# Weight sums of a Strassen-type product: from GpSimd instructions to an adding transfer

## Chip, cores and metric

One NeuronCore of a Trainium2 chip runs the whole program. The metric is the device time of one execution in microseconds (us). All data are float32; the products are made of float32r parts.

## What is computed

A trunk of four residual layers on 512 tokens of 1024 features, each layer a mixer followed by a SwiGLU feed-forward network, and one RMS norm at the end:

```python
for i in range(DEPTH):                       # 4 layers
    h = rmsnorm(x, norm_mix_g[i])
    m = short_conv(h) | spatial_gating(h) | retention(h)   # kinds 0, 1, 2, then 0 again
    x = x + m
    h = rmsnorm(x, norm_ffn_g[i])
    x = x + (silu(h @ w_gate) * (h @ w_up)) @ w_down       # 1024 -> 2816 -> 1024
return rmsnorm(x, final_norm_g)
```

The short convolution's input weights are 1024 x 3072, the gate and up weights 1024 x 2816 each.

## The kernel before

Every operand of a product is split into two float32r parts, high and low, and a product is three matmuls: high times high, high times low, low times high. `split` (lines 155 to 158) makes the parts: ScalarE casts to the high part, VectorE subtracts it from the source.

**Seven products for eight.** The convolution's input products and the gate and up products of the feed-forward networks use Winograd's form of Strassen's scheme: the weight matrix and the activations are cut in quarters, and seven products of quarters, or of sums of quarters, stand for eight. `columns7` makes 256 output features (a "chunk") that way: 7 parts of 12 matmuls, 84 matmuls of 256 columns. There are 104 such chunks: 20 in the two convolutions and 84 in the four feed-forward networks. The first chunk of each stage is made plainly by `columns4`, without sums.

**Weights.** `prepare7` (lines 114 to 140) prepares a chunk in two halves. For a half, SyncE loads 512 KB into a `raw` buffer (line 121; 4 buffers). The quarters lie in the order a11, a12, a22, a21. GpSimd makes three sums (lines 131 to 133), s1 = a21 + a22, s2 = s1 - a11 and s4 = a12 - s2, and VectorE makes s3 = a11 - a21 (line 134), all in a `sums` buffer (2 buffers, so one chunk). Then the three plain quarters of `raw` and the four sums are split (lines 157 and 158) into buffers of the pools `w7` and `wp`, which have four buffers each for either part, two chunks' worth. So the cast of a half waits until TensorE is done with the chunk before last, and the next sums wait until VectorE's subtraction has freed the `sums` buffer.

**Activations.** `operand_sums` (lines 381 to 396) makes the sums of quarters t1 to t4 of the activations for two blocks of features, four times in each stage that needs them: t1 and t3 by VectorE, t2 and t4 by GpSimd. `operand` (lines 366 to 376) scales and splits a block of x right after `leave` has added to it (line 422).

**Outcome.** `columns7` gathers the seven parts in three PSUM banks; ScalarE copies intermediate ones out (lines 227 to 243) and VectorE adds them (line 224). GpSimd also adds up squares for the norms (lines 302 to 307).

**Order.** A framework's scheduler orders each engine's instructions at build time by its own timeline; every engine then runs its list in order, and a transfer on SyncE's or GpSimd's queue waits in order too. `weights` prepares up to four chunks ahead, but at most one of the seven-part kind. In a feed-forward network the hidden blocks are made in four groups, (0,2), (2,5), (5,8), (8,11), a gate and an up chunk for each block; the down projection of one group (`leave`, eight blocks of 512-column matmuls) runs after the first gate chunk of the next. So four to six seven-part chunks follow each other between two down projections. In a convolution there are nine or eleven, with one small `leave` in between.

Of the kernel before, what the change touches and what calls it, by code (L numbers as in the profile page):

```python
# [17 lines left out]
P = 128  # L18
# [3 lines left out]
NB = D // P            # feature blocks of the residual stream  # L22
NT = T // P            # token blocks
FF = 2816
NF = FF // P
H = T // 2             # tokens of half the sequence
FF_PARTS = ((0, 2), (2, 5), (5, 8), (8, 11))  # pairs of hidden blocks, by part of an FFN
# [8 lines left out]
LAG = 3                # blocks of u that are ahead of the mixing of v  # L36
SOON = 100             # instructions that urgent ones may pass in the scheduler's order
BEGUN = 4              # blocks whose products begin before the last of their operands are ready
AHEAD = 4              # weight chunks prepared ahead of their matmuls


class Kernel:
# [18 lines left out]
    @contextmanager  # L61
    def dense(self):
        """Memory of the layers whose products take seven parts."""
        with (
            self.tc.tile_pool(name="w7", bufs=4, reuse_waits="tile") as self.w7,
            self.tc.tile_pool(name="sums", bufs=2, reuse_waits="tile") as self.sums,
            self.tc.tile_pool(name="hid", bufs=6, reuse_waits="tile") as self.hid,
            self.tc.tile_pool(name="own", bufs=1, reuse_waits="tile") as self.own,
        ):
            self.eye = self.diagonal(self.own.tile([P, P], F32, name="eye"))  # L70
            yield
        self.w7 = None

    @contextmanager
    def mixed(self):
        """Memory of the other layers."""
        with self.tc.tile_pool(name="blk", bufs=29, reuse_waits="tile") as self.blk:
            yield

# [17 lines left out]
    def plan7(self, src, plain=False):  # L97
        """Two blocks of columns, for columns4 if plain, else for columns7."""
        self.chunks.append((src, 0, plain))
# [14 lines left out]
    def prepare7(self, i):  # L114
        """Two blocks of columns, as the seven left operands of Winograd's form of Strassen's product."""
        nc = self.nc
        src, _, plain = self.chunks[i]
        out = [[] for _ in range(8)]
        for half in range(2):
            raw = self.raw.tile([P, NB // 4, 4, P], F32, tag="raw", name=f"raw{i}{half}")  # L120
            nc.sync.dma_start(raw, src[half])
            if plain:
                h, l = (self.wp.tile([P, NB // 4, 4, P], F32R, tag=part, name=f"w{part}{i}{half}") for part in "hl")
                self.split(raw, h, l)
                for j in range(4):
                    out[j] += [(h[:, k, j], l[:, k, j]) for k in range(NB // 4)]
                continue
            sums = self.sums.tile([P, NB // 4, 4, P], F32, tag="sums", name=f"sums{i}{half}")
            a11, a12, a22, a21 = (raw[:, :, j] for j in range(4))
            s1, s2, s3, s4 = (sums[:, :, j] for j in range(4))  # L130
            nc.gpsimd.tensor_add(s1, a21, a22)  # L131
            nc.gpsimd.tensor_sub(s2, s1, a11)  # L132
            nc.gpsimd.tensor_sub(s4, a12, s2)  # L133
            nc.vector.tensor_sub(s3, a11, a21)  # L134
            for x, n, first, pool in ((raw, 3, 0, self.w7), (sums, 4, 3, self.wp)):
                h, l = (pool.tile([P, NB // 4, n, P], F32R, tag=part, name=f"w{part}{i}{half}{n}") for part in "hl")
                self.split(x[:, :, :n], h, l)
                for j in range(n):
                    out[first + j] += [(h[:, k, j], l[:, k, j]) for k in range(NB // 4)]
        return out  # L140
# [14 lines left out]
    def split(self, src, h, l):  # L155
        """A float32 tile as two float32r tiles whose sum it is."""
        self.nc.scalar.copy(h, src)  # L157
        self.nc.vector.tensor_sub(l, src, h.bitcast(F32))  # L158
# [7 lines left out]
    def product(self, ps, terms, first=True, last=True, more=False):  # L166
        """ps (+)= sum of lhsT.T @ rhs over (lhs_h, lhs_l, rhs_h, rhs_l), the last term's at the end;
        more: added to a finished sum."""
        nc = self.nc
        seq = []  # L170
        for lh, ll, rh, rl in terms[:-1]:
            seq += [(lh, rh), (lh, rl)]
        seq += [(ll, rh) for lh, ll, rh, rl in terms[:-1]]
        lh, ll, rh, rl = terms[-1]
        seq += [(lh, rh), (lh, rl), (ll, rh)]
        for i, (x, y) in enumerate(seq):
            nc.tensor.matmul(  # L177
                ps, x, y, start=first and i == 0, stop=last and i == len(seq) - 1, skip_group_check=more
            )

    def columns(self, name, acts):
        """One block of output features (on partitions), for all tokens."""
# [14 lines left out]
    def begin(self, name, acts):  # L197
        """The start of columns(), with the weights of the rest."""
# [5 lines left out]
    def columns7(self, name, then, hold=False):  # L204
        """Two blocks of output features of the residual stream. then() gets them as [P, 2 * T], when the
        next product is under way."""
# [21 lines left out]
        part(c5, 3, xt, 0, True)  # L228
# [3 lines left out]
        part(c1, 4, xt, 1, False)  # L232
# [5 lines left out]
        part(c1, 5, xt, 2, False)  # L238
        add(y[:, 2 * H : 3 * H], c1, m5)

        def end():
            part(c1, 2, xt, 3, False)
            nc.scalar.copy(y[:, 3 * H :], c1)
# [4 lines left out]
    def columns4(self, name, then, hold=False):  # L248
        """The same by four products of blocks, for which the sums of the operand needn't be ready."""
# [16 lines left out]
    def finish(self, hold=False):  # L266
        """The rest of the last columns7, and what is done with its outcome (and those before it) unless on hold."""
# [8 lines left out]
    def rows(self, name, acts):  # L276
        """512 output features for each block of tokens (on partitions)."""
# [17 lines left out]
    def squares(self, src, add=None):  # L295
        """Running sum, over feature blocks, of the squares."""
# [12 lines left out]
    def rsqrt(self, ps, out, t):  # L309
        """out = ps ** -0.5, with a Newton step."""  # L310
# [7 lines left out]
    def scale_of(self, mean, r, t, *sums):  # L318
        """Each token's 1 / rms, on all partitions."""
# [8 lines left out]
    def diagonal(self, eye):  # L328
        """The matrix that mean_d is the inverse of, on vectors: D on the diagonal."""
# [8 lines left out]
    def scale_of_tokens(self, total):  # L338
        """Each token's 1 / rms, with tokens on partitions: a column for 128 of them."""
# [12 lines left out]
    def spread(self, r, t):  # L352
        """The same on all partitions, in PSUM."""
# [7 lines left out]
    def scale_in_psum(self):  # L361
        """Each token's 1 / rms, on all partitions."""
        return self.spread(self.scale_of_tokens(self.sum), self.hid.tile([P, 2 * T], F32, tag="hid", name="rs")[:, :T])

# [1 line left out]
    def operand(self, m, g):  # L366
        """x's block m as a part of the next product's operand."""
# [13 lines left out]
    def operand_sums(self, k, g):  # L381
        """The sums of quarters among the seven right operands, of two blocks of features."""
# [8 lines left out]
        nc.vector.tensor_sub(t1, b12, b11)  # L391
        nc.gpsimd.tensor_sub(t2, b22, t1)
        nc.vector.tensor_sub(t3, b22, b12)
        nc.gpsimd.tensor_sub(t4, b21, t2)
# [3 lines left out]
    def blocks(self):  # L398
        """The operand by single blocks of features."""
        return [(h[:, s], l[:, s]) for h, l in self.xs for s in (slice(0, T), slice(T, 2 * T))]  # L400

    def leave(self, acts, g, seven=False, final=True, midway=None, before=[], begun=()):
        """x += acts @ w; the next norm's gain is g. before: acts that begun products have already."""
# [26 lines left out]
    def end(self, acts):  # L430
        """The last layer's acts @ w on top of x, and the last norm, by halves of the tokens."""
# [37 lines left out]
    def last_norm(self, t, m):  # L469
        """Two blocks of features of half the tokens."""  # L470
# [14 lines left out]
    def normed(self, y, r):  # L485
        """y / rms, for two blocks"""
# [94 lines left out]
    def sgu(self, j, g, seven):  # L581
# [3 lines left out]
        # v, tokens on partitions  # L585
# [37 lines left out]
        # the causal mixing matrices, transposed: [s, group, t]  # L623
# [12 lines left out]
        # u, features on partitions, gated with the mixed v  # L636
# [32 lines left out]
    def retention(self, j, g, seven):  # L669
# [12 lines left out]
        for hd in range(HEADS):  # L682
# [28 lines left out]
            # scores, keys on partitions; of the last keys only 128 queries are left  # L711
# [79 lines left out]
    def plan_out(self, w, lo, hi):  # L791
        """All blocks of columns, of the blocks lo to hi of rows."""
# [84 lines left out]
def columns_by_two(w):  # L877
    """[n, K, M] as [n, M / 256, 2, P, K / 4 * 2]: two blocks of columns, half the rows at a time,
    rows on partitions, by pairs of blocks of rows."""
    n, k, m = w.shape  # L880
    w = w.reshape(n, 2, k // (4 * P), 2, P, m // (2 * P), 2, P).transpose(0, 5, 1, 4, 2, 6, 3, 7)
    return np.ascontiguousarray(w.reshape(n, m // (2 * P), 2, P, k // (4 * P), 4, P)[..., [0, 1, 3, 2], :])


def columns_first(w, parts=1):
    """[n, K, M] as [n, M / P, (parts,) P, K / P / parts * P]: one block of columns, rows on partitions."""
# [6 lines left out]
def rows_first(w):  # L893
    """[n, K, M] as [n, M / T, K / 256, P, 2 * T]: two blocks of rows of 512 columns."""
# [5 lines left out]
def tables():  # L900
    """Rotary angles and decays, by position and head alone."""
# [10 lines left out]
def by_partition(v):  # L912
    """[..., D] as [P, ... * D / P]."""
# [46 lines left out]
```

## Time and profile before

| | |
|---|---|
| time, median of 3 runs | 2485.07 us (2484.79 to 2485.66) |
| span of the profiled execution, first to last instruction | 2484.2 us |
| around the span (median less span; the profiled execution has no other time of its own) | 0.9 us |
| TensorE busy | 2417.6 us, 97% |
| VectorE busy | 1836.7 us, 74% |
| ScalarE busy | 1132.3 us, 46% |
| GpSimd busy | 890.0 us, 36% |
| mean granted TensorE clock | 0.994 of 2.4 GHz |

In rows of the profile, PE is TensorE, PEld its weight loads, DVE VectorE, ACT ScalarE, POOL GpSimd, and SP SyncE, which issues the loads. L134 is line 134 of the kernel. A name such as `wl<-sums,wh` says which tile is written from which. Times of instructions are in nanoseconds where the row says mean ns, all others in microseconds.

### The profile page before, as it was taken

The numbers are of one execution on the slowest core, as the hardware profiler recorded it, in microseconds if no ns is written. First come the engines' busy times: TensorE is split into PE (matmuls) and PEld (weight loads), VectorE is DVE, ScalarE is ACT, GpSimd is POOL, SyncE is SP. The second block draws the span as 40 slices with busy tenths as digits, with TensorE's granted clock in tenths as the row PEclk, the third lists the DMA queues.
The fourth block names the chain that finished last, engine by engine and source line by source line (L and its number), as shares of the span: only waits on it lengthen the run. The fifth ranks groups of instructions, "written<-read, shape, count | busy, mean of one in ns | idle before, by whom it ended". The sixth has DMA issues, their size and how long they took to land.

```text
span 2484.2 us, 37622 instructions
## 1 busy us (share of the span) xinstructions
PE 2417.6 (97%) x14892; PEld 2179.7 (88%) x14892; DVE 1836.7 (74%) x2236; ACT 1132.3 (46%) x1638; POOL 890.0 (36%) x788
## 2 busy tenths in 40 slices
PE   7999999999999999999999999999999899999998
PEld 6988989988888899998888888799999788889988
DVE  7988878763757887767565465988767898978776
ACT  6455445443324544534333334545435545545443
POOL 5536533520101643442000000834433744733530
PEclk9999999999999999999999999999999999999999
DMA  4141333334332233233223131233234124133231
GB/s 154 62 145 53 116 111 95 97 115 119 94 103 92 68 111 122 88 97 122 95 72 94 60 123 58 91 107 115 85 98 132 52 69 153 52 119 103 85 112 59
DMA packets 78832, 242.09 MB, mean 97 GB/s; under 512 B 8768, under 2 KB 12864, under 8 KB 78656
## 3 DMA queue, kind: packets, MB, share of 16 engines
q1 hardware_dynamic: 77568, 238.65, 30.3%
q8 instruction: 116, 1.90, 0.3%
q10 hardware_dynamic: 1088, 1.05, 0.1%
q14 instruction: 60, 0.49, 0.1%
HBM read 237.56 MB, written 2.10 MB: 96 GB/s over the span
## 4 chain that ended last, share of the span: by engine, by line
PE 75%; DVE 16%; issue 5%; ACT 2%; POOL 1%; DMA 0%; SPq 0%; DVEq 0%; ACTq 0%; POOLq 0%
PE out L177 26%; PE pu L177 16%; PE pg L177 15%; PE pv L177 7%; DVE wl L158 6%; PE pc L177 2%; PE q L177 2%; PE k L177 2%; PE pb L177 2%; DVE sums L134 2%; DVE puy L512 1%; PE pz L177 1%; DVE xl L375 1%; PE po L177 1%; DVE pgy L488 1%
## 5 line engine op out<-in xcount | busy, mean ns | idle before, releaser
L157 ACT CAST wh<-raw 128x768 fp32r<-128x768 f32 (+3 forms) x500 | 425.1, 858 | 572.5 <-PE out L177 193.5
L158 DVE TENSOR_TENSOR wl<-raw,wh 128x768 fp32r<-128x768 f32 (+3 forms) x500 | 557.6, 1134 | 136.7 <-ACT wh L157 136.3
L131 POOL TENSOR_TENSOR sums<-raw 128x256 f32<-128x256 f32 x208 | 243.3, 1170 | 795.8 <-DMA raw<-in_ffn_w_up 360.7
L157 ACT CAST wh<-sums 128x1024 fp32r<-128x1024 f32 x208 | 212.2, 1046 | 182.6 <-POOL sums L133 78.0
L177 PE MATMUL out<-hidl,wh 128*128 128x512 f32 (+1 forms) x736 | 278.3, 380 | 0.0
L158 DVE TENSOR_TENSOR wl<-sums,wh 128x1024 fp32r<-128x1024 f32 x208 | 260.9, 1279 | 22.1 <-ACT wh L157 18.8
L177 PE MATMUL out<-hidh,wh 128*128 128x512 f32 (+1 forms) x736 | 274.6, 381 | 0.0
L133 POOL TENSOR_TENSOR sums<-raw,sums 128x256 f32<-128x256 f32 x208 | 230.1, 1107 | 10.4
L132 POOL TENSOR_TENSOR sums<-sums,raw 128x256 f32<-128x256 f32 x208 | 217.9, 1048 | 10.6
L177 PE MATMUL pg<-xl,wh 128*128 128x256 f32 (+1 forms) x672 | 201.9, 316 | 9.6 <-DVE xl L375 9.6
L422 DVE TENSOR_TENSOR x<-out,x 128x512 f32<-128x512 f32 x192 | 130.2, 683 | 107.0 <-PE out L177 105.9
L177 PE MATMUL out<-hidh,wl 128*128 128x512 f32 (+1 forms) x736 | 205.4, 380 | 0.0
L177 PE MATMUL pg<-xh,wh 128*128 128x256 f32 (+1 forms) x672 | 200.9, 315 | 0.0
L177 PE MATMUL pu<-tl,wh 128*128 128x256 f32 x704 | 185.4, 284 | 5.1 <-DVE tl L158 5.1
L177 PE MATMUL pu<-xl,wh 128*128 128x256 f32 (+1 forms) x656 | 190.0, 306 | 0.0
L177 PE MATMUL pu<-xh,wh 128*128 128x256 f32 (+1 forms) x656 | 189.7, 306 | 0.0
L134 DVE TENSOR_TENSOR sums<-raw 128x256 f32<-128x256 f32 x208 | 153.3, 752 | 44.1 <-DMA raw<-in_ffn_w_up 37.9
L177 PE MATMUL pu<-th,wh 128*128 128x256 f32 x704 | 185.5, 285 | 0.0
L177 PE MATMUL pg<-th,wh 128*128 128x256 f32 x640 | 168.3, 284 | 6.9 <-DVE pgy L224 6.9
L177 PE MATMUL pg<-tl,wh 128*128 128x256 f32 x640 | 167.3, 283 | 0.0
L177 PEld LDWEIGHTS out<-hidl,wh 128*128 128x128 f32 x736 | 138.6, 188 | 25.1
L177 PEld LDWEIGHTS out<-hidh,wh 128*128 128x128 f32 x736 | 137.8, 188 | 25.0
(261 smaller groups left out, 6064.5 us busy)
## 6 DMA issues: line engine op xcount, KB each, us to landing
raw<-in_ffn_w_gate SPq DMA_DIRECT2D x88, 512.0 KB, 3.6
raw<-in_ffn_w_up SPq DMA_DIRECT2D x88, 512.0 KB, 3.6
raw<-in_ffn_w_down SPq DMA_DIRECT2D x96, 384.0 KB, 3.3
raw<-in_conv_w_in SPq DMA_DIRECT2D x48, 512.0 KB, 3.7
raw<-in_sgu_w_v SPq DMA_DIRECT2D x16, 512.0 KB, 3.6
raw<-in_sgu_w_u SPq DMA_DIRECT2D x16, 512.0 KB, 3.5
raw<-in_sgu_w_out SPq DMA_DIRECT2D x16, 512.0 KB, 3.5
raw<-in_ret_w_qk SPq DMA_DIRECT2D x16, 512.0 KB, 3.6
```

Source lines behind the costliest of these rows:

```text
L131: nc.gpsimd.tensor_add(s1, a21, a22)
L132: nc.gpsimd.tensor_sub(s2, s1, a11)
L133: nc.gpsimd.tensor_sub(s4, a12, s2)
L134: nc.vector.tensor_sub(s3, a11, a21)
L157: self.nc.scalar.copy(h, src)
L158: self.nc.vector.tensor_sub(l, src, h.bitcast(F32))
L177: nc.tensor.matmul(ps, x, y, start=first and i == 0, stop=last and i == len(seq) - 1, skip_group_check=more)
L375: nc.vector.scalar_tensor_tensor(l[:, s], x[:, s], gm, h[:, s].bitcast(F32), ALU.mult, ALU.subtract)
L422: nc.vector.tensor_add(x[:, s], ps, x[:, s])
L488: self.nc.vector.tensor_mul(y, y, r.unsqueeze(1).broadcast_to([P, 2, T]))
L512: nc.vector.tensor_mul(y[:, s], y[:, s], g[:, s])
```

## The change

The two sums of two quarters, a11 + a21 and a21 + a22, are no longer computed by an engine. SyncE loads the three plain quarters into `raw` (384 KB) and, with a second transfer, a21 twice into the first two places of `sums` (256 KB written). Then GpSimd's queue issues a transfer that adds a11 and a22 onto them while it writes (256 KB). VectorE makes the two longer sums from these with two additions. The signs are turned so that only additions are needed, which moves signs to the sums of activations (all four now on VectorE) and to two outcomes of `columns7`. The slots of the sums are renumbered, and the weights are laid out by quarters, so that a quarter's 256 numbers are contiguous in a row. The rest of the diff takes out comments.

```diff
     def prepare7(self, i):
@@
         for half in range(2):
-            raw = self.raw.tile([P, NB // 4, 4, P], F32, tag="raw", name=f"raw{i}{half}")
-            nc.sync.dma_start(raw, src[half])
             if plain:
+                raw = self.raw.tile([P, 4, NB // 4, P], F32, tag="raw", name=f"raw{i}{half}")
+                nc.sync.dma_start(raw, src[half])
...
-            sums = self.sums.tile([P, NB // 4, 4, P], F32, tag="sums", name=f"sums{i}{half}")
-            a11, a12, a22, a21 = (raw[:, :, j] for j in range(4))
-            s1, s2, s3, s4 = (sums[:, :, j] for j in range(4))
-            nc.gpsimd.tensor_add(s1, a21, a22)
-            nc.gpsimd.tensor_sub(s2, s1, a11)
-            nc.gpsimd.tensor_sub(s4, a12, s2)
-            nc.vector.tensor_sub(s3, a11, a21)
+            raw = self.raw.tile([P, 3, NB // 4, P], F32, tag="raw", name=f"raw{i}{half}")
+            sums = self.sums.tile([P, 4, NB // 4, P], F32, tag="sums", name=f"sums{i}{half}")
+            nc.sync.dma_start(raw, src[half][:, :3])
+            nc.sync.dma_start(sums[:, :2], src[half][:, 3:].broadcast_to([P, 2, NB // 4, P]))
+            nc.gpsimd.dma_start(sums[:, :2], src[half][:, :3:2], accum_op=ALU.add)
+            nc.vector.tensor_add(sums[:, 2], sums[:, 1], raw[:, 0])
+            nc.vector.tensor_add(sums[:, 3], sums[:, 2], raw[:, 1])
             for x, n, first, pool in ((raw, 3, 0, self.w7), (sums, 4, 3, self.wp)):
-                h, l = (pool.tile([P, NB // 4, n, P], F32R, tag=part, name=f"w{part}{i}{half}{n}") for part in "hl")
-                self.split(x[:, :, :n], h, l)
+                h, l = (pool.tile([P, n, NB // 4, P], F32R, tag=part, name=f"w{part}{i}{half}{n}") for part in "hl")
+                self.split(x, h, l)
@@ columns7
-        part(c5, 3, xt, 0, True)
+        part(c5, 4, xt, 0, True)
...
-        part(c1, 4, xt, 1, False)
+        part(c1, 5, xt, 1, False)
...
-        part(c1, 5, xt, 2, False)
-        add(y[:, 2 * H : 3 * H], c1, m5)
+        part(c1, 3, xt, 2, False)
+        with self.tc.high_priority(SOON):
+            nc.vector.scalar_tensor_tensor(y[:, 2 * H : 3 * H], c1, -1.0, m5, ALU.mult, ALU.subtract)
@@
-            nc.scalar.copy(y[:, 3 * H :], c1)
+            nc.scalar.mul(y[:, 3 * H :], c1, -1.0)
@@ operand_sums
-        nc.vector.tensor_sub(t1, b12, b11)
-        nc.gpsimd.tensor_sub(t2, b22, t1)
+        nc.vector.tensor_sub(t1, b11, b12)
         nc.vector.tensor_sub(t3, b22, b12)
-        nc.gpsimd.tensor_sub(t4, b21, t2)
+        nc.vector.scalar_tensor_tensor(t2, t1, -1.0, b22, ALU.mult, ALU.subtract)
+        nc.vector.scalar_tensor_tensor(t4, t2, -1.0, b21, ALU.mult, ALU.subtract)
```

## Rows read from the trace of the kernel before

**Rows 1.** Part 1 of the page: busy time and share of each engine.
```profile
PE 2417.6 (97%) x14892; PEld 2179.7 (88%) x14892; DVE 1836.7 (74%) x2236; ACT 1132.3 (46%) x1638; POOL 890.0 (36%) x788
```
**Rows 2.** Busy time by stretch: PE, PEld, DVE, ACT, POOL, then clock, DMA share, GB/s.
```profile
250.00:500.00 250.00, 248.50 (x1726) 232.95 (x1725) 194.66 (x234) 114.67 (x173) 111.79 (x102) 1.00 0.33 103
...
1950.00:2100.00 150.00, 142.52 (x1032) 134.16 (x1031) 128.79 (x160) 71.70 (x118) 71.44 (x61) 0.99 0.29 92
```
**Rows 3.** PE on the timeline inside a feed-forward network.
```profile
1029.53 0.28 PE L177 MATMUL pg<-th,wh 128*128 128x256 f32 x1
...
1029.65 0.28 PE L177 MATMUL pg<-tl,wh 128*128 128x256 f32 x1
```
**Rows 4.** The eight stretches around mixers and convolutions: columns as in rows 2, last their sum.
```profile
0.00:50.00 50.00, 38.35 (x169) 31.86 (x169) 40.76 (x42) 35.95 (x48) 27.33 (x30) 1.00 0.53 184
50.00:200.00 150.00, 143.66 (x958) 133.87 (x959) 135.56 (x165) 76.12 (x119) 73.64 (x60) 0.97 0.29 94
200.00:250.00 50.00, 46.30 (x338) 43.67 (x337) 42.45 (x50) 26.81 (x43) 27.05 (x23) 0.97 0.18 53
800.00:850.00 50.00, 47.54 (x242) 40.95 (x241) 41.79 (x43) 28.18 (x38) 38.76 (x36) 0.97 0.28 94
...
sum 640.00, PE 591.09 PEld 531.64 DVE 547.34 ACT 343.32 POOL 348.96; mean PE 73.89 PEld 66.45 DVE 68.42 ACT 42.92 POOL 43.62
```
**Rows 5.** PE's waits: who for whom, us in total, times, longest.
```profile
PE pg L177 <- DVE xl L375: 9.6, 8, 2.8
...
PE pg L177 <- DVE pgy L224: 6.9, 9, 0.9
```
**Rows 6.** Instructions on the tile `sums`: ns min/median/max, first and last start.
```profile
L134 DVE TENSOR_TENSOR sums<-raw x208: 407/948/1512, 21.6 to 2416.8; 128x256 f32<-128x256 f32 x104
...
L158 DVE TENSOR_TENSOR wl<-sums,wh x208: 1204/1217/2320, 37.1 to 2430.2; 128x1024 fp32r<-128x1024 f32 x104
```
**Rows 7.** Groups by form, whole span: count, busy us, mean ns, idle before.
```profile
L158 DVE TENSOR_TENSOR wl<-raw,wh 128x768 fp32r<-128x768 f32 x320 | 365.3, 1168 | 29.6 <-ACT wh L157 29.6
...
L134 DVE TENSOR_TENSOR sums<-raw 128x256 f32<-128x256 f32 x208 | 153.3, 752 | 44.1 <-DMA raw<-in_ffn_w_up 37.9 <-DMA raw<-in_conv_w_in 5.0
...
L375 DVE SCALAR_TENSOR_TENSOR xl<-x,gain,xh 128x512 fp32r<-128x512 f32 x64 | 71.5, 1142 | 8.3 <-ACT xh L374 8.3
```
**Rows 8.** DVE by form from 416 to 437, POOL idle there.
```profile
L158 DVE TENSOR_TENSOR wl<-raw,wh 128x768 fp32r<-128x768 f32 x8 | 7.4, 951 | 0.7 <-ACT wh L157 0.7
```
**Rows 9.** Timeline of the stretch 800 to 850: the same form without and beside POOL.
```profile
805.44 0.73 DVE L375 SCALAR_TENSOR_TENSOR xl<-x,gain,xh 128x512 fp32r<-128x512 f32 x1
...
807.57 1.23 DVE L375 SCALAR_TENSOR_TENSOR xl<-x,gain,xh 128x512 fp32r<-128x512 f32 x1
```
**Rows 10.** One round of the `sums` buffers, 1006 to 1036, engine by engine.
```profile
1008.83 2.35 DVE L158 TENSOR_TENSOR wl<-sums,wh 128x1024 fp32r<-128x1024 f32 x2
...
1010.12 1.65 POOL L131 TENSOR_TENSOR sums<-raw 128x256 f32<-128x256 f32 x1 [10.96 <-DVE wl L158]
...
1016.45 1.61 POOL L133 TENSOR_TENSOR sums<-raw,sums 128x256 f32<-128x256 f32 x1
...
1018.44 1.99 ACT L157 CAST wh<-sums 128x1024 fp32r<-128x1024 f32 x2
...
1019.71 2.35 DVE L158 TENSOR_TENSOR wl<-sums,wh 128x1024 fp32r<-128x1024 f32 x2
```
**Rows 11.** DMA issues: KB each, median us to landing.
```profile
raw<-in_ffn_w_gate SPq DMA_DIRECT2D x88, 512.0 KB, 3.6
...
raw<-in_ffn_w_down SPq DMA_DIRECT2D x24, 256.0 KB, 2.6
...
gb<-in_sgu_ln_g SPq DMA_DIRECT2D x4, 256.0 KB, 4.3
...
bs<-in_sgu_b_s SPq DMA_DIRECT2D x2, 256.0 KB, 7.2
```
**Rows 12.** SyncE's queue: its longest waits in total, times, longest.
```profile
SPq L121 <- DVE wl L158: 952.7, 202, 23.7
```

More of the change, by code (lines that the diff above doesn't have):

```diff
@@ L119, in prepare7 @@
         for half in range(2):
-            raw = self.raw.tile([P, NB // 4, 4, P], F32, tag="raw", name=f"raw{i}{half}")
-            nc.sync.dma_start(raw, src[half])
             if plain:
-                h, l = (self.wp.tile([P, NB // 4, 4, P], F32R, tag=part, name=f"w{part}{i}{half}") for part in "hl")
+                raw = self.raw.tile([P, 4, NB // 4, P], F32, tag="raw", name=f"raw{i}{half}")
+                nc.sync.dma_start(raw, src[half])
+                h, l = (self.wp.tile([P, 4, NB // 4, P], F32R, tag=part, name=f"w{part}{i}{half}") for part in "hl")
@@ L124, in prepare7 @@
                 self.split(raw, h, l)
                 for j in range(4):
-                    out[j] += [(h[:, k, j], l[:, k, j]) for k in range(NB // 4)]
+                    out[j] += [(h[:, j, k], l[:, j, k]) for k in range(NB // 4)]
                 continue
-            sums = self.sums.tile([P, NB // 4, 4, P], F32, tag="sums", name=f"sums{i}{half}")
-            a11, a12, a22, a21 = (raw[:, :, j] for j in range(4))
-            s1, s2, s3, s4 = (sums[:, :, j] for j in range(4))
-            nc.gpsimd.tensor_add(s1, a21, a22)
@@ L138, in prepare7 @@
                 for j in range(n):
-                    out[first + j] += [(h[:, k, j], l[:, k, j]) for k in range(NB // 4)]
+                    out[first + j] += [(h[:, j, k], l[:, j, k]) for k in range(NB // 4)]
         return out
@@ L880, in columns_by_two @@
     n, k, m = w.shape
-    w = w.reshape(n, 2, k // (4 * P), 2, P, m // (2 * P), 2, P).transpose(0, 5, 1, 4, 2, 6, 3, 7)
-    return np.ascontiguousarray(w.reshape(n, m // (2 * P), 2, P, k // (4 * P), 4, P)[..., [0, 1, 3, 2], :])
+    w = w.reshape(n, 2, k // (4 * P), 2, P, m // (2 * P), 2, P).transpose(0, 5, 1, 4, 6, 3, 2, 7)
+    return np.ascontiguousarray(w.reshape(n, m // (2 * P), 2, P, 4, k // (4 * P), P)[:, :, :, :, [0, 1, 3, 2]])
 def columns_first(w, parts=1):
```

## The prediction

> **What bounds the kernel.** First the busy times of the page [rows 1]: TensorE has work in 97% of the span, so 2484.2 - 2417.6 = 66.6 us are all that it visibly idles. Then the stretches. In the middle of a feed-forward network TensorE is busy 248.5 of 250 us [rows 2], and on the timeline 256-column matmuls start 0.12 us apart without a gap [rows 3]: a chunk takes 84 x 0.12 = 10.1 us and nothing behind TensorE is late. Nearly all idle time lies elsewhere. The eight stretches around mixers and convolutions hold 640 - 591.1 = 48.9 us of it, and there VectorE is busy 547.3 of 640 us, 86%, against 78% in the network [rows 2, 4]. The clock is seen in these stretches too: the granted mean is 0.97 in three rows, which are 250 us long [rows 4], so some 7 us of full speed are lost there, after stalls. Of the waits of TensorE the longest are for VectorE's splits (`xl`, 9.6 us) and its additions from PSUM (6.9 us in nine waits of 0.9 or less) [rows 5].
>
> Why VectorE is slow is read from single instructions. Line 134 takes 0.41 us at best and 0.95 in the median, in which GpSimd works on the same half [rows 6]. The split of 128x768 has a mean of 1.17 us, and 0.95 in a stretch without GpSimd [rows 7, 8]; `xl` takes 0.73 us in one place and 1.23 in another [rows 9], 1.14 in the mean [rows 7]. So GpSimd's sums, themselves not on TensorE's path, lengthen VectorE's work.
>
> **The change, part by part.**
>
> *GpSimd's 624 sum instructions go*, and 48 sums of activations go to VectorE. VectorE's splits of 128x768 get back up to 320 x (1.17 - 0.95) = 69 us, `xl` up to 64 x (1.14 - 0.73) = 26 us. Against that, line 134 with its mean of 0.752 us becomes two additions of 0.41: 208 x 0.07 = 15 us more; t2 and t4 add 48 x 0.41 = 20 us. Net some 60 us of 1837 less. In a chain this matters more than in the sum: t2 and t4 follow t1 without a change of engine.
>
> *What that is worth.* In the networks nothing, beyond part of the 6.9 us in small waits: TensorE sets the pace. In the eight stretches 48.9 us of idling and some 7 us of clock are at stake, of which 11.6 belong to the start, with the first loads [rows 4]. That leaves 44, with the small waits 51. I take half, 25 us: the rest is dependence that stays, since `xl` still follows an addition from PSUM and ScalarE's scaling. Its bounds are 0 and 51.
>
> *The way of a half through its `sums` buffer* becomes longer, and here the change can lose. In one round of today the buffers come free with two subtractions from 1008.8 on, GpSimd is at the sums until 1018.1, ScalarE casts at 1018.4 and VectorE subtracts at 1019.7: a round of 10.9 us [rows 10], of which the sums take some 5 for a half, and most of the rest is a wait for TensorE to free the `wp` buffers. New: copy of a21, 2.6 us (a load of 256 KB [rows 11]); the adding transfer, A; two additions, 0.82; cast, 1.0 (half of the 1.99 for two); subtraction, 1.22 [rows 6, 10]; and some 1.0 for standing in ScalarE's and VectorE's queues, my estimate from VectorE's share of 78%. That is 6.6 + A.
>
> A is in no row. Its bounds are the fastest and slowest loads of 256 KB, 2.6 and 7.2 us [rows 11]; a gain against a plain load is excluded, since the same bytes move and the target must be read besides. I take 4.3, the load of 256 KB in between [rows 11]. The round is then 10.9 us against TensorE's 10.1. A half is finished about 3.6 us after its cast could begin (1018.4 to 1022.1), and is needed a chunk later and behind the chunk's first part of 12 matmuls: a margin of 10.1 + 1.4 - 3.6, about 8 us. In the longest run of a network, six chunks between two down projections, five rounds eat 5 x 0.8 = 4 us of it, and the down projection refills it. So at A = 4.3 this costs nothing there. In a convolution, nine or eleven chunks run with one small interruption; VectorE, not TensorE, sets their pace, and I put 2 us on them.
>
> By the Trainium skill, page "DMA: Bandwidth & Descriptors", section "Anatomy of one DMA", a transfer from GpSimd takes 2.0 us plus bytes over 436 GB/s, an estimate of 2.6 us for these 256 KB. By it the round would be 9.2 us and the 2 us would fall away. No row of this kernel shows such a transfer.
>
> *SyncE and GpSimd's queues.* The one load of a half, 512 KB, becomes one of 384 and one writing 256, a third issue each on GpSimd. The DMA engines are busy a third of the time [rows 2], which hides it. But the copy of a21 waits for its `sums` buffer, and the next `raw` load stands behind it. Today SyncE already waits 952.7 us for `raw` buffers [rows 12] with no harm; the cover is the chunk prepared ahead. GpSimd's squares now stand behind transfers that wait for a landing; their sum is needed later, with the first gate outcome. Both at nothing.
>
> *Signs, slots, layout*: as many instructions of the same shapes on TensorE and ScalarE, nothing.
>
> **Sum.** 2484.2 - 25 + 2 = 2461.2 us of span, plus 0.9 around it (the median of the runs shown is 2485.07): **2462 us**. About 5 us, 0.2%, is what a measurement of this kernel can tell from no change.
>
> **Rivals.**
>
> 1. *The adding transfer is slow, and the round becomes the pace.* Five rounds cost more than the margin when 5 x (6.6 + A - 10.1) exceeds 8, from A = 5.1 on. There are eight such runs, two a network. The loss is 8 x (5 x (A - 3.5) - 8): at 5.7 it cancels the 23 us, at 6.5 it is 56 us, at 7.2 84. So 2462 + 56 = 2518 at 6.5 and 2546 at 7.2. For it: two dependent transfers per half where there was one load ahead of time. Against: the fast rows [rows 11] and DMA engines two thirds idle [rows 2].
>
> 2. *VectorE holds the transfer up.* If its issue has to wait for the VectorE instruction under way, up to 1.2 us [rows 6], A becomes 5.5; the loss is 16 us, and the time 2478, a third of the gain left. The trace shows the two engines in each other's way, for sums [rows 6]. By the Trainium skill, "SBUF — State Buffer", section "SBUF: two separate sides", a GpSimd transfer's descriptors wait while VectorE runs in a two-port mode; by its section "Who interferes with whom", instructions with two SBUF inputs, which nearly all of the rows here are, hinder only GpSimd's reads. No row shows which.
>
> 3. *The gain isn't there.* GpSimd stays in VectorE's way while it issues, or VectorE, in order, stands before an addition whose transfer is late, ahead of additions from PSUM. Then VectorE has only the 35 us more, and about half of what falls in the eight stretches, 5 us, shows; the time is 2485 to 2492. For it: VectorE already idles 44.1 us before line 134, nearly all of it for loads [rows 7].
>
> **Numbers.** The forecast has 0.56 (its own range 2442 to 2475), rival 1 0.24, rival 2 0.08, rival 3 0.12. Faster: the forecast, rival 2 and no part of the others, less a little for rounds that almost cancel, 0.60. Same: a third of rival 3 and the crossing of rival 1, 0.08. Slower: 0.32. The range of 2440 to 2535 takes in all of these but gains above 47 us and A beyond 6.9.
>
> **What would show it.** Right: the splits of 128x768 near 0.95 us everywhere, line 134's successors near 0.41, VectorE's total down by some 60 us, TensorE's idle sum in the eight stretches near 25. The transfer from issue to landing shows A; below 5 the subtractions of sums still end before TensorE asks. Wrong: TensorE waiting for `wl` of sums late in a run of six chunks, in the networks, growing from chunk to chunk (rival 1); VectorE idling before the two additions (rival 3); 1.1 us splits with GpSimd idle (another cause of the stretching).

## The result, and the profile after

The changed kernel takes 2642.18 us (2640.07 to 2650.65) against 2485.36 us (2484.79 to 2486.78) before: a ratio of 1.0636 [1.062, 1.0653], 157 us slower. The forecast was 2462 us, and even its range ended at 2535.

Part 1 of the page after, of a span of 2638.4 us, answers to [rows 1]:

```profile
PE 2465.8 (93%) x14892; PEld 2212.3 (84%) x14892; DVE 1735.5 (66%) x2492; ACT 1128.2 (43%) x1638; POOL 377.9 (14%) x324
```

VectorE and GpSimd work less than before, ScalarE about as much. TensorE makes the same 14892 matmuls, but idles 2638.4 - 2465.8 = 172.6 us where it idled 66.6, and its matmuls together take 48 us longer. So 154 us of span are 106 of idling and 48 of slower matmuls.

Where it is lost is seen by stage (a stage is one convolution's products, or the gate and up products of one feed-forward network), each from its first matmul on the timeline to its last. Busy time by stretch before: the two convolutions, then the four networks, then their sum (columns as in rows 2):

```profile
7.90:167.90 160.00, 149.91 (x982) 139.07 (x983) 147.22 (x173) 86.86 (x134) 78.71 (x64) 0.97 0.34 113
1928.00:2088.60 160.60, 146.26 (x1056) 136.78 (x1056) 141.83 (x170) 79.86 (x128) 84.58 (x70) 0.99 0.27 85
195.20:521.40 326.20, 321.01 (x2237) 300.93 (x2236) 256.10 (x307) 154.05 (x233) 142.00 (x128) 0.99 0.31 98
...
2115.70:2453.30 337.60, 329.47 (x2294) 307.91 (x2293) 258.46 (x304) 154.10 (x229) 141.39 (x128) 1.00 0.29 91
sum 1637.80, PE 1589.26 PEld 1487.26 DVE 1315.10 ACT 783.68 POOL 732.76; mean PE 264.88 PEld 247.88 DVE 219.18 ACT 130.61 POOL 122.13
```

The same stages after:

```profile
7.20:177.00 169.80, 153.49 (x983) 141.98 (x984) 127.33 (x196) 86.70 (x134) 24.72 (x22) 0.95 0.60 152
2048.00:2214.80 166.80, 149.85 (x1056) 139.59 (x1055) 125.14 (x191) 79.91 (x127) 32.97 (x28) 0.97 0.56 135
206.20:571.00 364.80, 333.63 (x2240) 310.10 (x2239) 238.39 (x350) 155.38 (x236) 51.62 (x46) 0.97 0.53 131
...
2244.70:2606.90 362.20, 337.78 (x2294) 313.97 (x2293) 240.06 (x347) 156.36 (x232) 51.52 (x46) 0.98 0.53 130
sum 1789.40, PE 1637.91 PEld 1521.76 DVE 1205.26 ACT 785.44 POOL 265.13; mean PE 272.99 PEld 253.63 DVE 200.88 ACT 130.91 POOL 44.19
```

The six stages hold 1789.4 - 1637.8 = 151.6 of the 154.2 us: 16 in the convolutions (336.6 against 320.6), 136 in the networks, in which TensorE had been busy nearly without a gap. VectorE's time there is 110 us less. The rest of the span is 849.0 us after and 846.4 before.

**The contention is gone for the weights, as forecast, and only in part for the activations.** VectorE's groups by form, after, answer to [rows 7]:

```profile
L159 DVE TENSOR_TENSOR wl<-raw,wh 128x768 fp32r<-128x768 f32 x320 | 300.3, 960 | 23.6 <-ACT wh L158 23.3
L134 DVE TENSOR_TENSOR sums<-sums,raw 128x256 f32<-128x256 f32 x208 | 87.9, 423 | 468.4 <-issue 264.4 <-DMA sums<-in_ffn_w_gate 85.4 <-DMA sums<-in_conv_w_in 58.3
L135 DVE TENSOR_TENSOR sums<-sums,raw 128x256 f32<-128x256 f32 x208 | 86.9, 420 | 2.6
L377 DVE SCALAR_TENSOR_TENSOR xl<-x,gain,xh 128x512 fp32r<-128x512 f32 x64 | 58.7, 935 | 8.0 <-ACT xh L376 8.0
```

The split of 128x768 has the 0.96 us that it had beside an idle GpSimd [rows 8], against 1.17 before, and the additions take 0.42. `xl` falls from 1.14 only to 0.94, where the forecast's upper bound took 0.73: half of its 26 us. But ahead of line 134 VectorE now idles 468 us, where it idled 44.

**What a half goes through.** The DMA issues of the networks after: KB each, median us to landing:

```profile
sums<-in_ffn_w_up SPq DMA_DIRECT2D x88, 256.0 KB, 2.9
sums<-in_ffn_w_up POOLq DMA_DIRECT2D x88, 256.0 KB, 4.9
sums<-in_ffn_w_gate SPq DMA_DIRECT2D x80, 256.0 KB, 2.9
sums<-in_ffn_w_gate POOLq DMA_DIRECT2D x80, 256.0 KB, 5.1
```

The timeline of one round after, all engines, answers to [rows 10] (x2 are two instructions in one row; `pg` and `pu` are the gate and up products in PSUM, `pgm` and `pgy` ScalarE's copies and VectorE's sums of them):

```profile
1080.90 1.51 SPq L132 DMA_DIRECT2D sums<-in_ffn_w_gate  x2
...
1084.36 2.27 POOL L133 DMA_DIRECT2D sums<-in_ffn_w_gate  x2 [11.07 <-DMA sums<-in_ffn_w_gate]
1084.80 0.41 DVE L225 TENSOR_TENSOR pgy<-pg,pgm 128x256 f32<-128x256 f32 x1
...
1089.09 0.42 DVE L134 TENSOR_TENSOR sums<-sums,raw 128x256 f32<-128x256 f32 x1 [3.88 <-issue]
1089.43 0.42 DVE L225 TENSOR_TENSOR pgy<-pg,pgm 128x256 f32<-128x256 f32 x1
1089.77 0.41 DVE L135 TENSOR_TENSOR sums<-sums,raw 128x256 f32<-128x256 f32 x1
1090.10 0.42 DVE L241 SCALAR_TENSOR_TENSOR pgy<-pg,pgm 128x256 f32<-128x256 f32 x1
1090.26 1.05 ACT L158 CAST wh<-sums 128x1024 fp32r<-128x1024 f32 x1 [4.30 <-DVE sums L135]
...
1090.57 0.39 PE L178 MATMUL pg<-th,wh 128*128 128x256 f32 x1 [1.53 <-DVE pgy L241]
...
1092.48 1.22 DVE L159 TENSOR_TENSOR wl<-sums,wh 128x1024 fp32r<-128x1024 f32 x1
...
1098.95 0.28 PE L178 MATMUL pg<-th,wh 128*128 128x256 f32 x1
```

The buffer comes free at 1080.9, and SyncE issues the copy at once; it lands at 1083.8. GpSimd issues the adding transfer at 1084.4; it lands at 1089.0. VectorE has had nothing to do since 1085.2: its list holds line 134 next, and behind it the additions of the product under way (lines 225 and 241). They run only from 1089.4 on, and TensorE, which needs the bank that line 241 reads, stands for 1.5 us. The cast follows at 1090.3, the subtraction ends at 1093.7, and the buffer is free again: a round of 12.8 us, the following ones 13.1 and 13.9. Two buffers hold the two halves of one chunk, so a chunk can be prepared once in a round. Against the 10.1 us that a chunk takes on TensorE, that is the pace. The releaser "issue" at line 134 is the wait for the transfer: over all 208 halves the first addition starts 0.08 us (median) after the landing.

TensorE's longest waits after answer to [rows 5]:

```profile
PE pu L178 <- DVE puy L241: 40.7, 21, 3.9
PE pg L178 <- DVE pgy L241: 30.9, 19, 2.9
PE pg L178 <- DVE xl L377: 11.9, 5, 5.1
```

The granted clock falls after some of these stalls. Three stretches of 5 us in the first network after:

```profile
415.00:420.00 5.00, 2.02 (x18) 1.82 (x16) 1.94 (x6) 0.92 (x1) 0.00 (x0) 1.00 0.37 52
420.00:425.00 5.00, 5.00 (x29) 5.00 (x30) 5.00 (x6) 2.62 (x6) 0.63 (x1) 0.66 0.49 135
425.00:430.00 5.00, 5.00 (x44) 5.00 (x43) 0.43 (x3) 1.05 (x1) 1.55 (x2) 1.00 1.01 223
```

TensorE stood for 3 us; in the next 5 us the granted clock is 0.66 in the mean, between the levels of 1.2 and 2.4 GHz, and 29 matmuls are made in place of 44. Not every stall does this: of 440 to 445 TensorE stood for 1.8 us, and the granted clock stays at 1.00 there and in the next 5 us.

### The profile page after: what moved, and what is told of

The parts are those of the page before. It is cut to its first block, busy times and chain, and to the rows that moved or that the text cites. A ratio compares the mean times of both kernels' runs of the same rounds, so it can differ in the third digit from the quotient of the medians.

```text
span 2638.4 us, 37764 instructions
## 1 busy us (share of the span) xinstructions
PE 2465.8 (93%) x14892; PEld 2212.3 (84%) x14892; DVE 1735.5 (66%) x2492; ACT 1128.2 (43%) x1638; POOL 377.9 (14%) x324
## 3 DMA queue, kind: packets, MB, share of 16 engines
q0 software_dynamic: 56576, 54.54, 14.0%
## 5 line engine op out<-in xcount | busy, mean ns | idle before, releaser
L159 DVE TENSOR_TENSOR wl<-raw,wh 128x768 fp32r<-128x768 f32 (+3 forms) x500 | 486.6, 988 | 123.5 <-ACT wh L158 123.0
L134 DVE TENSOR_TENSOR sums<-sums,raw 128x256 f32<-128x256 f32 x208 | 87.9, 423 | 468.4 <-issue 264.4
L159 DVE TENSOR_TENSOR wl<-sums,wh 128x1024 fp32r<-128x1024 f32 x208 | 253.8, 1229 | 18.3 <-ACT wh L158 12.9
L178 PE MATMUL pu<-th,wh 128*128 128x256 f32 x704 | 194.1, 295 | 49.7 <-DVE puy L241 40.7
L178 PE MATMUL pg<-th,wh 128*128 128x256 f32 x640 | 173.8, 291 | 40.2 <-DVE pgy L241 30.9
L178 PE MATMUL pu<-tl,wh 128*128 128x256 f32 x704 | 191.3, 290 | 2.6 <-DVE tl L159 2.5
L178 PEld LDWEIGHTS pu<-th,wh 128*128 128x128 f32 x704 | 139.7, 198 | 56.2 <-DVE puy L241 45.2
L133 POOL DMA_DIRECT2D sums<-in_ffn_w_up x88 | 95.9, 1101 | 555.0 <-DMA sums<-in_ffn_w_up 301.0
L133 POOL DMA_DIRECT2D sums<-in_ffn_w_gate x80 | 87.0, 1092 | 594.1 <-DVE wl L159 252.3
L178 PEld LDWEIGHTS pg<-th,wh 128*128 128x128 f32 x640 | 125.0, 195 | 46.7 <-DVE pgy L241 34.7
```

Source lines behind the costliest of these rows:

```text
L133: nc.gpsimd.dma_start(sums[:, :2], src[half][:, :3:2], accum_op=ALU.add)
L134: nc.vector.tensor_add(sums[:, 2], sums[:, 1], raw[:, 0])
L178: nc.tensor.matmul(ps, x, y, start=first and i == 0, stop=last and i == len(seq) - 1, skip_group_check=more)
```

## The experiments

**One plain load in place of both transfers.** The two short sums are replaced by one load from SyncE, and the addition of a21 is left out:

```diff
-            nc.sync.dma_start(sums[:, :2], src[half][:, 3:].broadcast_to([P, 2, NB // 4, P]))
-            nc.gpsimd.dma_start(sums[:, :2], src[half][:, :3:2], accum_op=ALU.add)
+            nc.sync.dma_start(sums[:, :2], src[half][:, :3:2])
```

> Leaves out the addition of a21: one plain load from SyncE puts a11 and a22 where the two short sums would stand; all else as in the changed kernel. Theory A (the two dependent transfers make a round of a sums buffer last 13.0 us where TensorE needs 10.1 a chunk; nothing else in the change costs): the round falls to 2.9 + 0.84 + 1.05 + 1.2 + about 1.5 of queues = 7.5 us, TensorE waits for line 241 vanish, and the time shows the gain of a GpSimd without sums, 2450 to 2475 us. Theory B (the extra bytes, the layout, the turned signs or the four sums of activations on VectorE cost most of it): 2550 us or more.

Measured: 2442.87 us (2441.25 to 2444.05), 0.9821 [0.9806, 0.9835] of the kernel before. Part 1 of its page:

```profile
PE 2405.0 (99%) x14892; PEld 2171.1 (89%) x14892; DVE 1746.3 (72%) x2492; ACT 1140.3 (47%) x1638; POOL 150.6 (6%) x116
```

That is 199 us less than the changed kernel takes: the whole loss lies in the two transfers; signs, layout, the longer additions and the activations' sums on VectorE, together, are not part of it. Without it the rest of the change gains 44 us (2486.60 to 2442.87), more than the 25 of the forecast.

**The same load from GpSimd's queue**, plain, still without the copy:

```diff
-            nc.sync.dma_start(sums[:, :2], src[half][:, 3:].broadcast_to([P, 2, NB // 4, P]))
-            nc.gpsimd.dma_start(sums[:, :2], src[half][:, :3:2], accum_op=ALU.add)
+            nc.gpsimd.dma_start(sums[:, :2], src[half][:, :3:2])
```

> Leaves out the addition of a21: as the first of these runs, but the plain load of a11 and a22 is issued by GpSimd. It measures what the queue costs without the adding. If the addition makes the transfer slow (target read as well), issue to landing falls from 5.0 to 3.5 us or less; if GpSimd's queue makes it slow, it stays at 4.5 to 5. Time in either case 2450 to 2480 us under A, since the round is then below 10.1 us.

Measured: 2458.65 us, once. Its DMA queues and issues:

```profile
q0 software_dynamic: 16640, 54.54, 7.3%
...
sums<-in_ffn_w_up POOLq DMA_DIRECT2D x88, 256.0 KB, 3.2
sums<-in_ffn_w_gate POOLq DMA_DIRECT2D x80, 256.0 KB, 3.1
```

The issues from SyncE in the run before this one:

```profile
sums<-in_ffn_w_up SPq DMA_DIRECT2D x88, 256.0 KB, 3.0
```

The first row in the changed kernel:

```profile
q0 software_dynamic: 56576, 54.54, 14.0%
```

For the same 54.54 MB the adding transfers take 56576 packets and 14.0% of the DMA engines in place of 16640 and 7.3%, and land after 5.0 us (median of all) in place of 3.15. So 1.8 us of a round are the adding, 0.15 the queue, and 2.9 + 0.6 the copy that must land first.

**The additions behind the product's.** The two longer sums are held in VectorE's order until line 241's last addition of the product under way:

```diff
-            nc.vector.tensor_add(sums[:, 2], sums[:, 1], raw[:, 0])
-            nc.vector.tensor_add(sums[:, 3], sums[:, 2], raw[:, 1])
+            with self.tc.issue_after(self.third.ins) if self.third else nullcontext():
+                nc.vector.tensor_add(sums[:, 2], sums[:, 1], raw[:, 0])
+                nc.vector.tensor_add(sums[:, 3], sums[:, 2], raw[:, 1])
...
-            nc.vector.scalar_tensor_tensor(y[:, 2 * H : 3 * H], c1, -1.0, m5, ALU.mult, ALU.subtract)
+            self.third = nc.vector.scalar_tensor_tensor(y[:, 2 * H : 3 * H], c1, -1.0, m5, ALU.mult, ALU.subtract)
```

> The two additions of a half are held behind the last third addition from PSUM (line 241) in VectorE's order; everything is computed. Theory A1 (it is VectorE's order that passes the late transfer on to TensorE: it stands before the additions while line 241 of an earlier chunk is ready behind them): TensorE's waits for line 241, 78 us in the changed kernel, fall below 20, and waits for wl of sums appear late in runs of six chunks; with a round of 13 us, a margin of 8 and eight runs that is some 60 to 90 us over 2462, so 2520 to 2580 us. Theory A2 (the weights are late anyway, the order does not matter): 2620 to 2660 us, the waits only change their name.

Measured: 2623.68 us (2622.02 to 2626.36), 1.0548 [1.053, 1.0565]. TensorE's waits there:

```profile
PE pu L179 <- ACT wh L159: 29.9, 13, 3.1
PE pg L179 <- DVE wl L160: 20.7, 11, 3.7
PE pg L179 <- ACT wh L159: 18.0, 19, 2.4
```

The waits for line 241 (here 242) fall from 79 to 6 us, and in their place TensorE waits for the splits of weights. Of 157 us this takes off 18. It is no clean price of the order, since the pinned additions start later: from one copy to the next into the same buffer 15.2 us pass in the networks (median), against 14.0 in the changed kernel. With either order the sums come late.

**The longer sums on GpSimd**, so that VectorE stands before no transfer: the two `nc.vector.tensor_add` become `nc.gpsimd.tensor_add`.

> The two longer sums are made by GpSimd from the transfer's two, so VectorE does not stand before the transfer. A1: TensorE's waits for line 241 below 20 us, but the round gets longer by GpSimd's slower additions and its own order (14 to 16 us): 2540 to 2620 us. A2: 2650 us or more.

Measured: 2647.33 us, once. ScalarE's longest wait there, and TensorE's:

```profile
ACT wh L158 <- POOL sums L135: 476.2, 141, 8.2
```

```profile
PE pu L178 <- ACT pum L228: 31.5, 23, 3.9
PE pg L178 <- ACT pgm L228: 26.3, 14, 3.7
```

Now ScalarE stands in order before its cast of the late sums, with the copies out of PSUM behind it. In these three orders of work the engine that takes up the late sum first passes the lateness on.

**All four sums on VectorE**, out of one load of 512 KB, with neither transfer:

```diff
-            raw = self.raw.tile([P, 3, NB // 4, P], F32, tag="raw", name=f"raw{i}{half}")
+            raw = self.raw.tile([P, 4, NB // 4, P], F32, tag="raw", name=f"raw{i}{half}")
...
-            nc.sync.dma_start(raw, src[half][:, :3])
-            nc.sync.dma_start(sums[:, :2], src[half][:, 3:].broadcast_to([P, 2, NB // 4, P]))
-            nc.gpsimd.dma_start(sums[:, :2], src[half][:, :3:2], accum_op=ALU.add)
+            nc.sync.dma_start(raw, src[half])
+            nc.vector.tensor_add(sums[:, :2], raw[:, :3:2], raw[:, 3:].broadcast_to([P, 2, NB // 4, P]))
...
-                self.split(x, h, l)
+                self.split(x[:, :n], h, l)
```

> The changed kernel with one load of 512 KB for a half, and VectorE making all four sums: one addition of a21 to a11 and a22 together (128x512, out of one load), then the two longer ones as in the changed kernel. No adding transfer, no copy of a21, nothing of the sums on GpSimd; the whole product is computed. Theory A (the loss is the round of copy, adding transfer and two additions through the two buffers): with the transfers gone the sums wait for nothing but the load, as in the run with one plain load, 2443 us; the extra addition is 208 x some 0.68 us = 141 us of VectorE, which has the time in the networks and not in the convolutions and around the mixers: 2450 to 2475 us, under the kernel before; TensorE idle under 60 us. Theory B (VectorE, with all sums and all splits, is itself the new bound, and the transfer only moved its waits): VectorE busy over 1870 us of the span, with additions from PSUM late, 2500 us or more.

Measured: 2459.14 us (2456.56 to 2459.93), 0.9889 [0.9875, 0.9904]. The added sum, by form:

```profile
L132 DVE TENSOR_TENSOR sums<-raw 128x512 f32<-128x512 f32 x208 | 142.4, 696 | 27.0 <-DMA raw<-in_ffn_w_up 23.8 <-DMA raw<-in_conv_w_in 2.5
```

VectorE takes 142 us more for it and is busy 1861 us, 76%, and the time rises by 16 us over the run with one plain load. VectorE's amount of work is not what slows the changed kernel.

**Four small buffers.** Copy and adding transfer stay. The tile holds only the two short sums, so that four fit into the same memory; `raw` is split first and then takes the longer sums:

```diff
-            self.tc.tile_pool(name="sums", bufs=2, reuse_waits="tile") as self.sums,
+            self.tc.tile_pool(name="sums", bufs=4, reuse_waits="tile") as self.sums,
...
-            sums = self.sums.tile([P, 4, NB // 4, P], F32, tag="sums", name=f"sums{i}{half}")
+            sums = self.sums.tile([P, 2, NB // 4, P], F32, tag="sums", name=f"sums{i}{half}")
...
+            self.split(raw, h, l)
...
+            nc.vector.tensor_add(raw[:, 0], sums[:, 1], raw[:, 0])
+            nc.vector.tensor_add(raw[:, 1], raw[:, 0], raw[:, 1])
...
+            self.split(sums, h[:, :2], l[:, :2])
+            self.split(raw[:, :2], h[:, 2:], l[:, 2:])
```

> The changed kernel with the same copy and the same adding transfer, but the sums tile holds only the two short sums (2 KB a partition), so that four fit where two did; the longer sums are written in place into raw, after raw has been split; the split of the seven sums' second part is done in two pieces. The whole product is computed. Theory A (two buffers: copy of the next half cannot start before the cast and subtraction of the half two earlier; the round of 13 to 14 us sets TensorE's pace in the networks): with four buffers the copy and the adding transfer run a chunk ahead, as far as the loads of raw do, the additions find their operand there, and the round as a limit doubles to some 26 us for two halves against 10 us that TensorE needs: 2450 to 2500 us, GpSimd's transfers still 4.5 to 6 us each. Theory C (it is the rate of adding transfers, 4.9 us each with one queue in order behind SP's copies, or VectorE's order, and not the number of buffers): 2590 us or more, with the waits before the two additions unchanged, some 300 us.

Measured: 2456.38 us (2453.69 to 2457.75), 0.9882 [0.9865, 0.9898]: 186 us faster than the changed kernel and 30 faster than the one before. Its page, parts 1 and 6, and then a row of its groups by form:

```profile
PE 2410.7 (98%) x14892; PEld 2174.6 (89%) x14892; DVE 1740.9 (71%) x2700; ACT 1162.1 (47%) x1846; POOL 396.9 (16%) x324
...
sums<-in_ffn_w_up POOLq DMA_DIRECT2D x88, 256.0 KB, 5.6
...
sums<-in_ffn_w_gate POOLq DMA_DIRECT2D x80, 256.0 KB, 6.1
```

```profile
L138 DVE TENSOR_TENSOR raw<-sums,raw 128x256 f32<-128x256 f32 x208 | 86.3, 426 | 1.9 <-DMA sums<-in_ffn_w_up 1.3
```

The adding transfers are even slower, 5.6 to 6.1 us, and it costs nothing: the sums lie there 18 us (median) before VectorE takes them up, which idles 1.9 us ahead of this addition where it idled 468.

**Four small buffers and the pinned additions** together:

> The run with four small buffers, and in addition the two longer additions held behind the third addition from PSUM of the product under way in VectorE's order. Theory A with A2 (VectorE standing in order before an addition whose transfer is late passes the lateness on): with four buffers nothing is late any more, so the order hardly matters: within 10 us of the run with four buffers alone. If four buffers alone leave a good part of the wait (over 2520 us there), this one is 15 to 20 us faster, as the same pin was on two buffers (18 us).

Measured: 2455.44 us (2452.47 to 2458.32), 0.9876 [0.9861, 0.9891], the same as without the pin. With nothing late the order has no price.

**Two and three small buffers.** `bufs=4` of that run becomes 2, then 3; nothing else differs.

> The run with small buffers and longer sums in place, with two buffers in place of four; nothing else differs. It tells the number of buffers from the other edits of that run. Theory A (the round through two buffers sets the pace): copy 2.9 + 0.6 to the issue + 5 to 6 for the adding transfer + an addition 0.4, cast 0.6, subtraction 0.7 and the places in the queues, some 11 to 12 us a chunk against TensorE's 10.1: slower than four buffers by 50 to 180 us, 2510 to 2640 us, with long waits of VectorE or ScalarE for the transfers. Theory D (the gain came from writing the longer sums in place and splitting raw first, so that the queues no longer stand before a late sum): 2450 to 2470 us, as with four.

> The same with three buffers. Theory A: a round of 12 to 14 us through three buffers serves two halves in 8 to 9.3 us, less than TensorE's 10.1 us for a chunk, so it is no limit any more: within 15 us of the run with four buffers, 2450 to 2472 us. Under theory C (a rate of transfers, not the buffers) it would lie as far from two buffers as four does only by chance.

Measured: 2639.36 us (2635.14 to 2646.98) with two, 1.0616 [1.0601, 1.0632], the changed kernel's time again; 2574.85 us (2569.85 to 2581.67) with three, 1.0352 [1.0334, 1.0371]. So the gain of four is the number of buffers and not the writing in place. ScalarE's waits with two:

```profile
ACT wh L162 <- DMA sums<-in_ffn_w_gate: 238.1, 72, 8.3
...
ACT wh L162 <- DMA sums<-in_ffn_w_up: 123.9, 48, 5.9
```

Three missed my figure by 100 us. I had divided the round by the buffers, as if halves came evenly. Timeline with three:

```profile
1043.47 0.41 DVE L138 TENSOR_TENSOR raw<-sums,raw 128x256 f32<-128x256 f32 x1
1043.96 0.38 SPq L132 DMA_DIRECT2D sums<-in_ffn_w_gate  x1
1044.37 0.62 ACT L162 CAST wh<-sums 128x512 fp32r<-128x512 f32 x1 [1.88 <-PE pg L182]
...
1047.27 1.09 POOL L133 DMA_DIRECT2D sums<-in_ffn_w_gate  x1 [13.88 <-ACT pum L232]
...
1051.40 0.62 ACT L162 CAST wh<-sums 128x512 fp32r<-128x512 f32 x1 [2.81 <-DMA sums<-in_ffn_w_gate]
```

Both halves of a chunk are taken up together. The first was loaded long ago and is cast at 1044.4; the second gets its buffer only when the chunk before has freed one, at 1043.9, and is cast at 1051.4, on its landing. One half of each chunk still goes through copy, transfer and wait with nothing ahead. That this is all of the 118 us against four buffers I read from the timeline alone.

**t2 and t4 back on GpSimd**, on top of four small buffers, 48 instructions of 128x256 (not 128x512, as the expectation says). Here t2 comes out with the opposite sign, and t4 from it as neither t4 nor its negative, so this run does not compute the product. It prices only the engine on which these instructions run; their number and shape are the same.

```diff
-        nc.vector.scalar_tensor_tensor(t2, t1, -1.0, b22, ALU.mult, ALU.subtract)
-        nc.vector.scalar_tensor_tensor(t4, t2, -1.0, b21, ALU.mult, ALU.subtract)
+        nc.gpsimd.tensor_add(t2, t1, b22)
+        nc.gpsimd.tensor_add(t4, t2, b21)
```

> The run with four small buffers, with the two sums of activations t2 and t4 back on GpSimd, as the kernel before has them (48 instructions of 128x512); the weights' sums stay as in the run with four buffers. It prices this part of the change alone. If much of the gain lies in the chain t1, t2, t4 without a change of engine ahead of the operand's split: 8 us or more slower than the run with four buffers, 2464 us or more. If the gain lies in GpSimd's 624 sums no longer lengthening VectorE's work: within 5 us of it, 2451 to 2461 us.

Measured: 2466.66 us (2465.97 to 2470.97), 0.9922 [0.991, 0.9935]: 10 us slower than with them on VectorE. They take 1.2 to 1.35 us each on GpSimd and 0.42 to 0.65 on VectorE. So of the 30 us that four buffers gain over the kernel before, some 10 come with the place of these two sums, and 20 with what else the change does.

## Why the prediction was wrong

**The step that failed** is "The round is then 10.9 us against TensorE's 10.1", with "a margin of 10.1 + 1.4 - 3.6, about 8 us" that was to cover it, "So at A = 4.3 this costs nothing there". Both halves of it were off:

- *The round.* Copy 2.6 forecast, 2.9 measured. Between the copy's landing and the issue that waits for it I put nothing; it is 0.56 (median). A was taken as 4.3 and measures 4.9 to 5.1. The additions, cast, subtraction and queues were 4.0 in sum, and are 4.7 in the round shown (1089.0 to 1093.7). None is a large miss, but all lie in one chain: 12.8 to 13.9 in place of 10.9, an excess over TensorE of 2.7 to 3.8 us in place of 0.8. That this is the cause is shown by the number of buffers: two small ones give 2639 us, four 2456.
- *The margin.* The weights of the round shown are split at 1093.7 and 1094.9 and used from 1099.0 on (the matmul with `th` in the timeline): 4 us are left of the 8. In the five chunks from 1072 on, until the next down projection, the later split ends 6.7, 5.1, 4.0, 1.1 and 0.4 us before the first use, so the margin is eaten up within one run of chunks. And TensorE stands before that: VectorE takes up line 134 of the next chunk in its list ahead of line 241 of this one, so the lateness reaches TensorE by a way on which the margin does not count.
- *The sum.* By the medians in the networks the chain is 2.9 + 0.6 + 5.0 + 4.4 = 12.9 us (4.4 from the first addition to the end of the subtraction). With five rounds of 12.9 the prediction's own sum gives 8 x (5 x 2.8 - 8) = 48 us with its margin and 8 x 5 x 2.8 = 112 without it. The networks lost 136. The sum leaves out the shorter runs of chunks and the clock; how the 136 divide between the way over line 241 and the eaten margin stays open, as the pinned run changes the round too.
- *The clock.* I priced no slower matmuls after new stalls. In the six stages matmuls take 1637.9 - 1589.3 = 49 of 152 us more. Some 35 of these are clock: by the granted clock while TensorE is busy, 47 us of full speed are lost there after and 12 before. The other 14 are not accounted for.

**Rival 1** named the mechanism and its break point, 5.1, where A then lay; its price at that A was about nothing, as it used the same round and margin. **Rival 3** named VectorE standing in order ahead of the additions from PSUM; it priced this at a gain forgone; taking it away in the pinned run gave 18 us. In the changed kernel that is the largest way by which the late round reaches TensorE, which waits 79 us for line 241 in all. **Rival 2** came nearer to A with 5.5, for a reason that the runs don't bear out: GpSimd's issue takes 1.09 us in the median beside a busy VectorE, and the plain transfer from the same queue lands in 3.15.

The estimate by the Trainium skill, "DMA: Bandwidth & Descriptors", section "Anatomy of one DMA", was 2.6 us for this transfer. Plain it took 3.1 to 3.2, half a microsecond more, and adding 4.9 to 5.1: it is no price for an adding transfer.

**The 2 us for the convolutions** were 16.

**The gain of 25** was right in kind and too low: 44 us with one plain load, 30 with four buffers and the whole work done. The contention row (0.96 in place of 1.17) came as forecast, `xl` by half, and VectorE's total fell by 101 us where I had 60.

**Both queues "at nothing"** holds with four buffers: the same issues stand in them, and TensorE idles 41 us. With two buffers no run takes the queues' order out alone.

## What to carry to other kernels

When a step of a ring of buffers becomes a chain of transfers, add up one buffer's whole way, with the time between one transfer's landing and the issue of the next, and set it against the pace of the bound: a round that is too long costs its excess in every turn once the margin is eaten, and here a second transfer of 5.6 to 6.1 us cost nothing once a whole work item (two halves) lay ready ahead. If the new step needs only part of the buffer, make the buffer that small and take more of them. Count a margin on every way to the bound engine, not only at the last consumer: an in-order engine can meet the late operand earlier, ahead of work that the bound engine needs.

## What was not expected of the hardware

An adding transfer took 272 packets for 256 KB (56576 / 208) where a plain one from the same queue took 80, twice the time of the DMA engines, and 1.8 us more to landing. Moving the plain 256 KB from SyncE's to GpSimd's queue cost 16 us in all (2442.87 to 2458.65, the latter measured once), though each lands only 0.15 us later; the cause of that was not looked for.
